# Operands of a mixer step laid out in DRAM as the core reads them: weights as packed tiles, x channel-major, vectors as columns

## The chip, the cores and the metric

The kernel runs on one core of one Trainium2 chip. A core has a matrix engine (TensorE, PE in the profile; its weight loads are PEld), a vector engine (VectorE, DVE), an activation engine (ScalarE, ACT), GpSimd (POOL) and a queue engine (SyncE, SP) that issues transfers to 16 DMA engines. All data are float32 in DRAM. The metric is device time in microseconds (us); lower is better.

## What is computed

One step of a two-layer diffusion backbone on 128 context tokens and 256 denoising tokens (384 together), width 2048. Each layer modulates a normalized x, projects it to eleven chunks of 512 channels, mixes four of the branches in different ways, gates each and projects back:

```python
shift, scale, gate = split(silu(cvec) @ w_mod[l] + b_mod[l], 3)
h = rmsnorm(x, norm_g[l]) * (1 + scale) + shift
(f_x, f_g, p_x, p_g, q, k, v, a_g, c_a, c_b, c_g) = split(h @ w_in[l], 11)
y_f = fourier_mix(f_x, w_fourier[l]) * silu(f_g)
y_p = pool_mix(p_x, w_pool[l], pool_scale[l]) * silu(p_g)
y_c = conv_module(c_a, c_b, ..., w_conv_pw[l]) * silu(c_g)
y_a = rmsnorm(diff_attention(q, k, v, lam), subln_g[l]) * silu(a_g)
x = x + gate * (concat(y_f, y_p, y_a, y_c) @ w_out[l])
```

`cvec` is `c_ctx` for the context tokens and `c` for the others. Denoising tokens attend to a cache of 128 keys and values besides their own, with rotary embedding. The outputs are the final RMS norm of both groups and the context's keys and values of both layers.

## The kernel before, in words

**Layouts.** On the chip x, h and all branches are channel-major: 128 channels on the partitions, the 384 tokens along the row, in four tiles (P, 4, 384) per tensor. Every large matmul runs as three (`mm3`, L483 to L486): weights and activations are each split into a high part in the fast float32r format and a low part with the rest (`halves`, L262; the split is an ACT copy, L113, and a DVE subtraction, L104).

**Weights.** `wtile` (L278) loads two blocks of 128 rows by 512 columns of a weight matrix as one raw tile of 512 KB, source rows of 2 KB each (`w_src`, L291), and splits it. There are five raw tiles and six high and low tiles in turn. w_mod comes three ways: `mod_item` (L304) for TensorE, in tiles (P, nk, nb, 128), one transfer for each of shift and scale, with rows of 512 bytes for one block, 1 KB for two, 2 and 4 KB for the wide ones; `side_item` (L362) for VectorE, which multiplies and adds raw rows; both are spread over the main stream by `pump` (L396) at rates set by hand (`set_rate`). In the last quarter of the output projection w_out comes in tiles (P, 8, 128), rows of 512 bytes.

**The start (L138 to L199, L838).** SP's queue is held in program order until the end of the lead stage (`manual_schedule`, closed at L881); elsewhere a planner orders every engine's instructions by priority, data flow and its own estimate of durations, and `ahead()` raises the priority of weight loads and splits. SP issues the constants' first 128 columns, two rows of conditioning vectors, then x by column groups of 512 in token-major form (two transfers a group) with norm_g and b_mod after the first group. TensorE transposes the conditioning vectors, then x block by block (48 transposes, L190), and norm_g and b_mod (L194, L195); ACT squares x with a running sum along the row (L110), DVE copies the transposes to xT (L191). The row sums give the RMS factor, which TensorE broadcasts (`bcast_tokens`, L457, matmul at L462).

**Lead stage of layer 0 (L849 to L879).** It goes through the 16 blocks of channels in groups of one, one, and then two. In each group TensorE computes shift and scale of the next (`mod_item`, matmul at L326), VectorE and ScalarE make h (`make_h`, L471), and four chunks (C_B, C_A, K, Q) get their part, added up in SBUF. x is also written to a DRAM copy `xd` (`keep_x`, L176), from which the residual is read back at the layer's end (L950). After the last group `late_vectors` (L214) loads the remaining constants and eight groups of vectors as rows and transposes them, and `make_lambda` (L238) broadcasts the lambda vectors with a matmul (L242).

**Attention's keys (`keys`, L624).** A generator that is stepped once per weight tile of the values chunk: it loads the cached keys token-major, transposes the new context keys on TensorE (L631), copies and stores them (L633, L634), transposes the cached keys (L638, L639), then rotates k and q (`rope`, L612).

**The rest.** The other chunks, the four mixers and their gates, and the output projection, where DVE adds the gated result to the residual (L107, tile xr).

Of the kernel before, what the change touches and what calls it, by code (L numbers as in the profile page):

```python
# [32 lines left out]
CONST_PARTS = [  # L33
    ("ident", 128),
    ("cdft", 256),
# [16 lines left out]
def mixer_step(  # L52
    ctx: ExitStack,
    tc: tile.TileContext,
    x_prompt, x_sample, cache_k, cache_v, c, c_ctx, norm_g, w_mod, b_mod, w_in,
    w_fourier, w_pool, pool_scale, diff_lambda, subln_g, conv_dw, conv_dw_b,
    conv_ln_g, conv_ln_b, w_conv_pw, w_out, final_g, consts,
# [39 lines left out]
    def cvtile(s):  # L97
        return cvp.tile([P, 4, 432], F32, tag="cv", name=nm(s))
# [42 lines left out]
    def load_rows(dst, rows):  # L141
        where, o = {}, 0
        for n, ap, k in rows:
            nc.sync.dma_start(out=dst[o:o + k], in_=ap)
            where[n] = o
            o += k
        return where, o
# [4 lines left out]
    load_rows(crow[:, 0:P], [("c_ctx", c_ctx.rearrange("(r p) -> r p", p=P), KC),  # L152
                             ("c", c.rearrange("o (r p) -> (o r) p", p=P), KC)])
    xtok = []
    nb = DEPTH * 3 * KC
    for g in range(4):
        xt = gtile("H", "xtok", (P, TB, BR))
        sl = slice(g * BR, (g + 1) * BR)
        nc.sync.dma_start(out=xt[:, 0, :], in_=x_prompt[0, :, sl])
        nc.sync.dma_start(out=xt[:, 1:3, :], in_=x_sample[0, :, sl].rearrange("(b p) c -> p b c", p=P))  # L160
        xtok.append(xt)
        if g == 0:
            where1, n1 = load_rows(crow[:, P:2 * P], [("norm_g", norm_g.rearrange("l (r p) -> (l r) p", p=P), DEPTH * KC)])
            nc.sync.dma_start(out=crow[:nb, 2 * P:3 * P], in_=b_mod.rearrange("l (r p) -> (l r) p", p=P))

# [1 line left out]
    cps = sm("cps")  # L167
# [6 lines left out]
    xd = [[drp.tile([P, 4, NT], F32, tag=f"xd{l}{g}", name=f"xd{l}{g}") for g in range(4)] for l in range(DEPTH)]  # L174

    def keep_x(l, g, t):  # L176
        nc.sync.dma_start(out=xd[l][g], in_=t)

    xT = []
    ssq = one.tile([P, TB, 4], F32, tag="ssq", name="ssq")  # L180
    junk = cvtile("junk").rearrange("p a b -> p (a b)")
    for g in range(4):
        xt = xtok[g]
        xT.append(gtile("X", "xT"))
# [8 lines left out]
    vps = sm("vps")  # L193
    nc.tensor.transpose(vps[:, 0:n1], crow[:n1, P:2 * P], ident[:n1, :n1])  # L194
    nc.tensor.transpose(vps[:, P:P + nb], crow[:nb, 2 * P:3 * P], ident[:nb, :nb])  # L195
    ncol = one.tile([P, n1], F32, tag="ncol", name="ncol")
    nc.vector.tensor_copy(out=ncol, in_=vps[:, 0:n1])
    bcol = one.tile([P, nb], F32, tag="bcol", name="bcol")
    nc.vector.tensor_copy(out=bcol, in_=vps[:, P:P + nb])  # L199

# [1 line left out]
    rows2 = [("final_g", final_g.rearrange("(r p) -> r p", p=P), KC),  # L202
             ("dw_b", conv_dw_b.rearrange("l (r p) -> (l r) p", p=P), 8),
             ("ln_g", conv_ln_g.rearrange("l (r p) -> (l r) p", p=P), 8),
             ("ln_b", conv_ln_b.rearrange("l (r p) -> (l r) p", p=P), 8),
             ("pscale", pool_scale.rearrange("l (r p) -> (l r) p", p=P), 8),
             ("subln", subln_g, DEPTH)]
    n2 = sum(r[2] for r in rows2)
    ndw = CONV_W * 4
    vcol = one.tile([P, n2], F32, tag="vcol", name="vcol")  # L210
    dwc = one.tile([P, DEPTH, CONV_W, 4], F32, tag="dwc", name="dwc")
    off = {}

    def late_vectors():  # L214
        nc.sync.dma_start(out=cst[:, o1:], in_=consts[:, o1:])
        vrow = kvp.tile([P, 512], F32, tag="kv", name="vrow")
        w2, _ = load_rows(vrow[:, 0:P], rows2)
        off.update(w2)
        for l in range(DEPTH):
            nc.sync.dma_start(out=vrow[:ndw, (1 + l) * P:(2 + l) * P],  # L220
                              in_=conv_dw[l].rearrange("t (b p) -> (t b) p", p=P))
        vps = sm("vps2")
        nc.tensor.transpose(vps[:, 0:n2], vrow[:n2, 0:P], ident[:n2, :n2])
        nc.vector.tensor_copy(out=vcol, in_=vps[:, 0:n2])
        for l in range(DEPTH):
            s0 = (1 + l) * P
            nc.tensor.transpose(vps[:, s0:s0 + ndw], vrow[:ndw, s0:s0 + P], ident[:ndw, :ndw])
            nc.vector.tensor_scalar(out=dwc[:, l].rearrange("p t b -> p (t b)"), in0=vps[:, s0:s0 + ndw],
                                    scalar1=0.5, scalar2=None, op0=ALU.mult)

    def col(n, i, k=1):
        return vcol[:, off[n] + i:off[n] + i + k]

# [4 lines left out]
    def make_lambda():  # L238
        lrow = gtile("X", "lrow", (P, 512))
        nc.sync.dma_start(out=lrow[0:1, :], in_=diff_lambda.rearrange("(o l) f d -> o (l f d)", o=1))  # L240
        lps = sm("lps")
# [15 lines left out]
    prio = [None]  # L257

    def ahead():
# [31 lines left out]
    def w_src(w2d, k0, c0, nk=2):  # L291
        return w2d[k0 * P:(k0 + nk) * P, c0:c0 + 512].rearrange("(k p) n -> p k n", p=P)
# [809 lines left out]
```

## Time and profile before

| | |
|---|---|
| three timed runs | 1274.0, 1268.66, 1265.95 us; median 1268.66 |
| span of the profiled execution | 1264.2 us |
| own time of the profiled execution beyond the span | not given on the page |
| mean granted TensorE clock | 0.992 |
| TensorE, VectorE, ScalarE busy | 97%, 73%, 44% |
| moved by DMA | 254.75 MB, mean 202 GB/s |

The span runs from the first to the last instruction of the profiled execution. "Busy" is the time in which an engine executes; a matmul's end is modelled, so two that overlap in the engine's pipeline count once. The chain is followed back from the last instruction, at each step to what released it.

### The profile page before, as it was taken

The numbers are of one execution on the slowest core, as the hardware profiler recorded it, in microseconds if no ns is written. First come the engines' busy times: TensorE is split into PE (matmuls) and PEld (weight loads), VectorE is DVE, ScalarE is ACT, GpSimd is POOL, SyncE is SP. The second block draws the span as 40 slices with busy tenths as digits, with TensorE's granted clock in tenths as the row PEclk, the third lists the DMA queues.
The fourth block names the chain that finished last, engine by engine and source line by source line (L and its number), as shares of the span: only waits on it lengthen the run. The fifth ranks groups of instructions, "written<-read, shape, count | busy, mean of one in ns | idle before, by whom it ended". The sixth has DMA issues, their size and how long they took to land.

```text
span 1264.2 us, 22313 instructions
## 1 busy us (share of the span) xinstructions
PE 1229.3 (97%) x8576; PEld 1144.0 (90%) x8576; DVE 923.1 (73%) x1795; ACT 557.7 (44%) x1128; POOL 2.1 (0%) x34
## 2 busy tenths in 40 slices
PE   6999999999999999999999999999999999999995
PEld 4888988798998999989998999979999999999995
DVE  4767686899995966998877559998455795657452
ACT  5422233345447545422235533334554765344442
POOL 0000000000000000000000000000000000000000
PEclk8999999999999999999999999999999999999998
DMA  9999997653446865989965444454323573545322
GB/s 273 333 314 310 297 321 268 205 183 117 140 160 201 284 233 188 315 295 310 322 212 184 154 163 150 151 160 137 121 83 110 171 253 117 184 164 188 122 69 100
DMA packets 159343, 254.75 MB, mean 202 GB/s; under 512 B 9019, under 2 KB 67973, under 8 KB 159238
## 3 DMA queue, kind: packets, MB, share of 16 engines
q1 hardware_dynamic: 159238, 253.34, 61.4%
q8 instruction: 67, 1.10, 0.4%
q14 instruction: 38, 0.31, 0.1%
HBM read 242.82 MB, written 10.49 MB: 200 GB/s over the span
## 4 chain that ended last, share of the span: by engine, by line
PE 86%; DVE 6%; DMA 4%; issue 2%; ACT 1%; SPq 1%; DVEq 0%; ACTq 0%
PE mm L484 23%; PE mm L486 22%; PE mm L485 22%; PE mod L326 4%; DVE lo L104 2%; PE mm L515 2%; PE mm L516 2%; PE mm L517 2%; DMA raw<-in_w_in_dram 2%; DVE cacc L107 1%; DMA mraw<-in_w_mod_dram 1%; PE sp L484 1%; PE sp L485 1%; PE scs L700 1%; PE sp L486 1%
## 5 line engine op out<-in xcount | busy, mean ns | idle before, releaser
L113 ACT ACTIVATE hi<-raw 128x512 fp32r<-128x512 f32 x498 | 308.5, 630 | 552.6 <-PE mm L485 341.1
L104 DVE TENSOR_TENSOR lo<-raw,hi 128x512 fp32r<-128x512 f32 x498 | 337.7, 689 | 216.0 <-ACT hi L113 203.7
L484 PE MATMUL mm<-hh,hi 128*128 128x384 f32 x1280 | 440.7, 345 | 6.6 <-DVE acc L104 3.4
L485 PE MATMUL mm<-hl,hi 128*128 128x384 f32 x1280 | 433.0, 338 | 0.0
L486 PE MATMUL mm<-hh,lo 128*128 128x384 f32 x1280 | 430.6, 339 | 0.4 <-DVE lo L104 0.4
L484 PEld LDWEIGHTS mm<-hh,hi 128*128 128x128 f32 x1280 | 240.7, 188 | 28.2 <-issue 12.2
L485 PEld LDWEIGHTS mm<-hl,hi 128*128 128x128 f32 x1280 | 242.0, 189 | 1.4 <-issue 0.8
L486 PEld LDWEIGHTS mm<-hh,lo 128*128 128x128 f32 x1280 | 241.2, 189 | 2.1 <-DVE lo L104 1.1
L484 PE MATMUL mm<-yh,hi 128*128 128x384 f32 x512 | 173.4, 340 | 3.9 <-DVE xr L107 3.9
L485 PE MATMUL mm<-yl,hi 128*128 128x384 f32 x512 | 172.4, 337 | 0.0
L486 PE MATMUL mm<-yh,lo 128*128 128x384 f32 x512 | 172.3, 337 | 0.0
L107 DVE SCALAR_TENSOR_TENSOR macc<-sraw,cmod,macc 128x512 f32<-128x512 f32 x210 | 147.7, 746 | 9.4 <-DMA sraw<-in_w_mod_dram 9.3
L107 DVE SCALAR_TENSOR_TENSOR cacc<-u,dwc,cacc 128x399 f32<-128x399 f32 x232 | 146.6, 632 | 5.3 <-ACT cacc L110 1.0
L484 PEld LDWEIGHTS mm<-yh,hi 128*128 128x128 f32 x512 | 96.2, 188 | 7.7 <-issue 6.1
L485 PEld LDWEIGHTS mm<-yl,hi 128*128 128x128 f32 x512 | 96.3, 188 | 0.0
L486 PEld LDWEIGHTS mm<-yh,lo 128*128 128x128 f32 x512 | 96.2, 188 | 0.0
L104 DVE TENSOR_TENSOR acc<-acc,mm 128x384 f32<-128x384 f32 x128 | 65.7, 552 | 24.1 <-PE mm L486 24.0
L326 PE MATMUL mod<-mraw,cmod 128*32 128x128 f32 (+2 forms) x1920 | 79.0, 294 | 3.3 <-DMA mraw<-in_w_mod_dram 2.6
L326 PEld LDWEIGHTS mod<-mraw,cmod 128*32 128x32 f32 x1920 | 48.5, 112 | 27.9 <-issue 16.0
L515 PE MATMUL mm<-hi,hh 128*128 128x512 f32 x96 | 38.4, 400 | 0.0
L516 PE MATMUL mm<-lo,hh 128*128 128x512 f32 x96 | 38.1, 397 | 0.0
L517 PE MATMUL mm<-hi,hl 128*128 128x512 f32 x96 | 37.9, 395 | 0.0
(232 smaller groups left out, 944.1 us busy)
## 6 DMA issues: line engine op xcount, KB each, us to landing
raw<-in_w_in_dram SPq DMA_DIRECT2D x172, 512.0 KB, 3.6
mraw<-in_w_mod_dram SPq DMA_DIRECT2D x72, 512.0 KB, 3.7
mraw<-in_w_mod_dram SPq DMA_DIRECT2D x128, 256.0 KB, 6.7
raw<-in_w_out_dram SPq DMA_DIRECT2D x64, 512.0 KB, 6.0
sraw<-in_w_mod_dram SPq DMA_DIRECT2D x56, 512.0 KB, 5.3
xr<-xd SPq DMA_DIRECT2D x8, 768.0 KB
xd<-xT SPq DMA_DIRECT2D x4, 768.0 KB
xd<-xr SPq DMA_DIRECT2D x4, 768.0 KB
```

What stands on the lines that cost most here:

```text
L104: (eng or nc.vector).tensor_tensor(out=out, in0=a, in1=b, op=op)
L107: nc.vector.scalar_tensor_tensor(out=out, in0=a, scalar=s, in1=b, op0=op0, op1=op1)
L113: nc.scalar.activation(out=out, in_=a, func=AF.Copy, scale=scale)
L326: nc.tensor.matmul(ps[qs, 0:nb * 32].rearrange("p (b n) -> p b n", n=32), lhsT=cmod[:, k0 + j, :], rhs=raw[:, j, :, qs], start=(k0 + j == ...
L484: nc.tensor.matmul(ps, lhsT=wh, rhs=ah, start=start, stop=False)
L485: nc.tensor.matmul(ps, lhsT=wh, rhs=al, start=False, stop=False)
L486: nc.tensor.matmul(ps, lhsT=wl, rhs=ah, start=False, stop=stop)
L515: nc.tensor.matmul(ps3[t], lhsT=hh[g][:, kb, ts], rhs=hi(j), start=st, stop=False)
L516: nc.tensor.matmul(ps3[t], lhsT=hh[g][:, kb, ts], rhs=lo(j), start=False, stop=False)
L517: nc.tensor.matmul(ps3[t], lhsT=hl[g][:, kb, ts], rhs=hi(j), start=False, stop=sp)
L700: nc.tensor.matmul(scs[qb, m][:, cs], lhsT=qs, rhs=kk[ms])
```

## The change

The host lays the operands out; the kernel's loads become plain copies. Each weight matrix becomes a flat array (`Pack`) in which the tiles stand one after the other in the order in which the program traces their loads, each tile with the bytes of a partition in one run: 4 KB per partition for a tile of 512 KB, for w_mod's shift and scale together in one transfer. x arrives channel-major (P, 4, 384) per tile. All vectors are columns of the constants, and those needed early stand with the identity matrix in the first load. The squares of x are summed over channels by TensorE with a column of ones. The DRAM copy of layer 0's x goes: its residual is read from the input. Cached keys arrive transposed, new keys leave as they stand on the chip (the host turns them), and lambda comes as 128 equal rows.

```diff
+VEC_EARLY = [("c_ctx", KC), ("c", KC), ("norm_g", DEPTH * KC), ("b_mod", DEPTH * 3 * KC)]
+VEC_LATE = [("final_g", KC), ("dw_b", 8), ("ln_g", 8), ("ln_b", 8), ("pscale", 8), ("subln", DEPTH),
+            ("dw", DEPTH * CONV_W * 4)]
-    o1 = CONST_OFF["cdft"][0]
+    o1 = CONST_OFF["ident"][0] + P
     nc.sync.dma_start(out=cst[:, :o1], in_=consts[:, :o1])
-    crow = kvp.tile([P, 512], F32, tag="kv", name="crow")
-    load_rows(crow[:, 0:P], ...)
...
+        xT.append(gtile("X", "xT"))
+        nc.sync.dma_start(out=xT[g], in_=x_in[g])
...
-    nc.tensor.transpose(cps[:, 0:2 * KC], crow[:2 * KC, 0:P], ident[:2 * KC, :2 * KC])
-    act(cmod[:, :, 0], cps[:, 0:KC], AF.Silu)
-    act(cmod[:, :, 1], cps[:, KC:2 * KC], AF.Silu)
+    act(cmod[:, :, 0], cview("c_ctx"), AF.Silu)
+    act(cmod[:, :, 1], cview("c"), AF.Silu)
+    ssq = sm("ssq")
     for g in range(4):
-        for t in range(TB):
-            act(junk[:, t * BR:(t + 1) * BR], xt[:, t, :], AF.Square, accum_out=ssq[:, t, g:g + 1])
+        xsq = gtile("M", "xsq0")
         for b in range(4):
-            ps = sm("xps")
+            act(xsq[:, b, :], xT[g][:, b, :], AF.Square)
             for t in range(TB):
-                nc.tensor.transpose(ps[:, t * P:(t + 1) * P], xt[:, t, b * P:(b + 1) * P], ident)
-            nc.vector.tensor_copy(out=xT[g][:, b, :], in_=ps[:, :NT])
+                nc.tensor.matmul(ssq[:, t:t + 1], lhsT=xsq[:, b, t * P:(t + 1) * P], rhs=ones[:, 0:1],
+                                 start=g == 0 and b == 0 and t == 0, stop=g == 3 and b == 3 and t == TB - 1)
+    dwc = cview("dw").rearrange("p (l t b) -> p l t b", l=DEPTH, b=4)
     def late_vectors():
         nc.sync.dma_start(out=cst[:, o1:], in_=consts[:, o1:])
-        vrow = kvp.tile([P, 512], F32, tag="kv", name="vrow")
...
+        nc.vector.tensor_scalar(out=cview("dw"), in0=cview("dw"), scalar1=0.5, scalar2=None, op0=ALU.mult)
     def make_lambda():
-        nc.tensor.matmul(lps, lhsT=ones[0:1, :], rhs=lrow[0:1, :])
-        lbc = gtile("X", "lbc", (P, 512))
-        nc.vector.tensor_copy(out=lbc, in_=lps)
+        lbc = kvp.tile([P, DEPTH * 4 * 64], F32, tag="kv", name="lbc")
+        nc.sync.dma_start(out=lbc, in_=lam)
-    def w_src(w2d, k0, c0, nk=2):
-        return w2d[k0 * P:(k0 + nk) * P, c0:c0 + 512].rearrange("(k p) n -> p k n", p=P)
+    def w_src(name, l, k0, c0, nk=2, n=512):
+        def rows(a):
+            return a[l, k0 * P:(k0 + nk) * P, c0:c0 + n].reshape(nk, P, n).transpose(1, 0, 2)
+        return packs[name].take(rows, (P, nk, n))
     def mod_item(l, segs, k0, nk):
...
-                nc.sync.dma_start(
-                    out=raw[:, :, o:o + n, :],
-                    in_=w_mod[l, k0 * P:(k0 + nk) * P, c0:c0 + n * P].rearrange("(k p) (b n) -> p k b n", p=P, n=P))
+            nc.sync.dma_start(out=raw, in_=packs["w_mod"].take(rows, (P, nk, nb, P)))
     def keys(l, k, q, kc):
-        ck = gtile("X", "ck", (P, 4, P))
         with ahead():
-            nc.sync.dma_start(out=ck, in_=cache_k[0, l].rearrange("h t d -> t h d"))
+            nc.sync.dma_start(out=kc, in_=cache_k[l])
         yield
-        for h in range(4):
-            nc.tensor.transpose(ps[:, h, :], k[:, h, 0:SEQ], ident)
-        ko = gtile("X", "ko", (P, 4, P))
-        nc.scalar.copy(out=ko, in_=ps)
-        nc.sync.dma_start(out=new_k[0, l].rearrange("h t d -> t h d"), in_=ko)
-        yield
-        ps = sm("ckT", (P, 4, P))
-        for h in range(4):
-            nc.tensor.transpose(ps[:, h, :], ck[:, h, :], ident)
-        nc.scalar.copy(out=kc, in_=ps)
+        nc.sync.dma_start(out=new_k[l], in_=k[:, :, 0:SEQ])
         yield
-                if k0 % 4 + nk == 4:
-                    keep_x(0, k0 // 4, xT[k0 // 4])
-            nc.sync.dma_start(out=xr[g], in_=xd[l][g])
+            nc.sync.dma_start(out=xr[g], in_=x_in[g] if l == 0 else xd[g])
+class Pack:
+    def take(self, rows, shape):
+        n = math.prod(shape)
+        flat = self.ap[self.at:self.at + n]
+        self.at += n
+        self.parts.append(rows)
+        if len(shape) == 3:
+            return flat.rearrange("(p a b) -> p a b", p=shape[0], a=shape[1])
+        return flat.rearrange("(p a b c) -> p a b c", p=shape[0], a=shape[1], b=shape[2])
```

## Rows read from the trace of the kernel before

**Rows 1.** The page: span, busy time of each engine, the chain by engine.

```profile
span 1264.2 us, 22313 instructions
...
PE 1229.3 (97%) x8576; PEld 1144.0 (90%) x8576; DVE 923.1 (73%) x1795; ACT 557.7 (44%) x1128; POOL 2.1 (0%) x34
...
PE 86%; DVE 6%; DMA 4%; issue 2%; ACT 1%; SPq 1%; DVEq 0%; ACTq 0%
...
```

**Rows 2.** Windows: stretch, us, busy us of each engine (instructions), granted clock, DMA share, GB/s.

```profile
...
2.00:4.00 2.00, 0.28 (x1) 0.18 (x1) 0.00 (x0) 1.86 (x5) 0.00 (x0) 1.00 0.42 91
4.00:8.00 4.00, 1.99 (x8) 1.59 (x9) 0.36 (x1) 1.83 (x5) 0.00 (x0) 1.00 0.87 257
8.00:12.00 4.00, 3.14 (x14) 2.14 (x13) 2.07 (x5) 2.02 (x7) 0.00 (x0) 1.00 1.00 292
12.00:14.00 2.00, 2.00 (x11) 1.50 (x10) 1.66 (x4) 1.41 (x5) 0.00 (x0) 1.00 1.06 402
14.00:20.00 6.00, 4.84 (x87) 3.47 (x85) 5.09 (x15) 4.33 (x12) 0.41 (x6) 1.00 1.20 299
28.00:31.00 3.00, 3.00 (x18) 2.56 (x20) 0.46 (x1) 1.51 (x4) 0.00 (x0) 0.50 1.15 296
66.00:74.00 8.00, 8.00 (x96) 6.97 (x96) 4.64 (x13) 3.19 (x6) 0.00 (x0) 1.00 1.05 384
...
```

**Rows 3.** Timeline of the start: start, us, engine, line, operation, count, idle before.

```profile
...
7.31 10.70 SPq L315 DMA_DIRECT2D mraw<-in_w_mod_dram  x8
...
23.54 1.08 PE L326 MATMUL mod<-mraw,cmod 128*32 128x64 f32 x32
...
24.69 0.25 DVE L331 STREAM_TRANSPOSE T<-mod 128x64 f32<-128x64 f32 x1 [4.87 <-PE mod L326]
...
27.27 0.80 PE L484 MATMUL mm<-hh,hi 128*128 128x384 f32 x3 [1.33 <-ACT hh L110]
...
```

**Rows 4.** The chain in order of time, at the start: start, us, what.

```profile
...
15.44 5.46 DMA mraw<-in_w_mod_dram
...
22.03 1.58 PE bc L462 x2
...
```

**Rows 5.** TensorE waits to 230 us (three), after (one): us total, times, longest.

```profile
...
PE mm L484 <- DVE acc L104: 3.4, 3, 1.9
PE mod L326 <- DMA mraw<-in_w_mod_dram: 0.7, 2, 0.5
PE mm L486 <- DVE lo L104: 0.4, 1, 0.4
...
PE mm L484 <- DVE xr L107: 3.9, 4, 1.6
...
```

**Rows 6.** The chain between 150 and 157 us.

```profile
...
150.37 6.41 DMA raw<-in_w_in_dram
...
```

**Rows 7.** Timeline of TensorE around the transposes of layers 0 and 1.

```profile
...
224.47 0.40 PE L515 MATMUL mm<-hi,hh 128*128 128x512 f32 x1
...
226.56 0.48 PE L516 MATMUL mm<-lo,hh 128*128 128x512 f32 x1
...
229.96 0.66 PE L638 MATMUL ckT<-cst,ck 128*128 128x128 f32 x4
...
827.43 0.60 PE L631 MATMUL kT<-cst,k 128*128 128x128 f32 x4
...
```

**Rows 8.** Squares by tile (ns min/median/max); row sums and broadcast on the chain.

```profile
...
L110 ACT ACTIVATE xsq<-xr x30: 507/524/527, 561.8 to 1250.8; 128x384 f32<-128x384 f32 x30
...
673.97 0.83 PE st L467 x6
...
676.65 0.86 PE bc L462 x2
...
```

**Rows 9.** Layer 1: SP after the key store; landing of the values' store.

```profile
...
829.81 10.07 SPq L266 DMA_DIRECT2D raw<-in_w_in_dram  x3
...
DMA to landing us min/median/max: 4.5/4.5/4.5
...
```

More of the change, by code (lines that the diff above doesn't have):

```diff
@@ L54, in mixer_step @@
     tc: tile.TileContext,
[L55 to L57 removed]
+    x_in, cache_k, cache_v, consts, lam, packs,
     y_prompt, y_sample, new_k, new_v,
@@ L154, in mixer_step @@
-    xtok = []
-    nb = DEPTH * 3 * KC
-    for g in range(4):
[L157 to L164, printed above, removed]
@@ L171, in mixer_step @@
     warm = one.tile([P, 1], F32, tag="warm", name="warm")
     act(warm, cmod[:, 0, 2:3], AF.Sqrt, bias=eps_t[:, 0:1])
[L174 to L181, printed above, removed]
+    ncol = cview("norm_g")
+    bcol = cview("b_mod")
+    xd = [drp.tile([P, 4, NT], F32, tag=f"xd{g}", name=f"xd{g}") for g in range(4)]
@@ L193, in mixer_step @@
[L193 to L207, printed above, removed]
@@ L215, in late_vectors @@
         nc.sync.dma_start(out=cst[:, o1:], in_=consts[:, o1:])
-        vrow = kvp.tile([P, 512], F32, tag="kv", name="vrow")
[L217 to L229, printed above, removed]
+        nc.vector.tensor_scalar(out=cview("dw"), in0=cview("dw"), scalar1=0.5, scalar2=None, op0=ALU.mult)
     def col(n, i, k=1):
-        return vcol[:, off[n] + i:off[n] + i + k]
+        return cview(n)[:, i:i + k]
@@ L311, in mod_item, with rows @@
         with ahead():
-            o = 0
-            for kind, b0, n in segs:
-                c0 = MOD.index(kind) * D + b0 * P
-                nc.sync.dma_start(
-                    out=raw[:, :, o:o + n, :],
-                    in_=w_mod[l, k0 * P:(k0 + nk) * P, c0:c0 + n * P].rearrange("(k p) (b n) -> p k b n", p=P, n=P))
-                o += n
+            def rows(a):
+                parts = []
+                for kind, b0, n in segs:
+                    c0 = MOD.index(kind) * D + b0 * P
+                    parts.append(a[l, k0 * P:(k0 + nk) * P, c0:c0 + n * P].reshape(nk, P, n, P))
+                import numpy as np
+                return np.concatenate(parts, axis=2).transpose(1, 0, 2, 3)
+            nc.sync.dma_start(out=raw, in_=packs["w_mod"].take(rows, (P, nk, nb, P)))
         key = (l, segs)
@@ L370, in side_item @@
         with ahead():
-            nc.sync.dma_start(out=raw, in_=w_src(w_mod[l], k0, c0))
+            nc.sync.dma_start(out=raw, in_=w_src("w_mod", l, k0, c0))
         for j in range(2):
@@ L531, in small_proj @@
         ah, al = src
-        wt = [wtile(w_src(src2d, 2 * kt, 0)) for kt in range(2)]
+        wt = [wtile(w_src(name, l, 2 * kt, 0)) for kt in range(2)]
         for b in range(4):
@@ L811, in pool_proj @@
             yield
-        hi, lo = wtile(w_pool[l].rearrange("g c d -> c g d"), shape=(P, 4, P))
+        hi, lo = wtile(packs["w_pool"].take(lambda a: a[l].transpose(1, 0, 2), (P, 4, P)), shape=(P, 4, P))
         for g in range(4):
@@ L834, in evac4 @@
         return t
-    ssum = tiny.tile([P, TB], F32, tag="ssum", name="ssum")
-    nc.vector.tensor_reduce(out=ssum, in_=ssq, axis=AX.X, op=ALU.add)
-    stat = ssum
+    stat = ssq[:, 0:TB]
     for l in range(DEPTH):
@@ L932, in mixer_step @@
         mix_p = gtile("M", "mixp")
-        ft = start(small_proj(w_fourier[l], fm, lambda b, ps: nc.scalar.copy(out=mix_f[:, b, :], in_=ps), WF))
+        ft = start(small_proj("w_fourier", l, fm, lambda b, ps: nc.scalar.copy(out=mix_f[:, b, :], in_=ps), WF))
         pt = start(pool_proj(l, px, mix_p))
@@ L941, in mixer_step @@
         mix_c = gtile("M", "mixc")
-        ct = start(small_proj(w_conv_pw[l], cs, lambda b, ps: nc.scalar.copy(out=mix_c[:, b, :], in_=ps), WC))
+        ct = start(small_proj("w_conv_pw", l, cs, lambda b, ps: nc.scalar.copy(out=mix_c[:, b, :], in_=ps), WC))
         gate(C_G, Y_C, mix_c, ct)
@@ L1068, in shape_constants, with __init__, array, channel_columns @@
     parts["edge"] = np.broadcast_to(edge.reshape(1, 64), (P, 64))
[L1069 to L1076 removed]
+    return parts
+WEIGHTS = ("w_in", "w_mod", "w_out", "w_fourier", "w_pool", "w_conv_pw")
+_OUTS = [((1, SEQ, D), "float32"), ((1, DEC, D), "float32"), ((DEPTH, P, 4, SEQ), "float32"),
+         ((DEPTH, SEQ, BR), "float32")]
+class Pack:
+    def __init__(self, ap, size):
+        self.ap, self.size, self.at, self.parts = ap, size, 0, []
+    def take(self, rows, shape):
+        n = math.prod(shape)
+        assert self.at + n <= self.size
+        flat = self.ap[self.at:self.at + n]
[4 more added lines that the diff above has]
+        return flat.rearrange("(p a b c) -> p a b c", p=shape[0], a=shape[1], b=shape[2])
+    def array(self, a):
+        import numpy as np
+        assert self.at == self.size
+        return np.concatenate([np.ascontiguousarray(rows(a)).ravel() for rows in self.parts])
+def channel_columns(i):
+    import numpy as np
+    def cols(a):
+        return np.asarray(a, np.float32).reshape(-1, P).T
+    parts = {"c_ctx": cols(i["c_ctx"]), "c": cols(i["c"]), "norm_g": cols(i["norm_g"]), "b_mod": cols(i["b_mod"]),
+             "final_g": cols(i["final_g"]), "dw_b": cols(i["conv_dw_b"]), "ln_g": cols(i["conv_ln_g"]),
+             "ln_b": cols(i["conv_ln_b"]), "pscale": cols(i["pool_scale"]), "subln": cols(i["subln_g"]),
+             "dw": cols(i["conv_dw"])}
+    parts.update(shape_constants())
+    return np.ascontiguousarray(np.concatenate([parts[n] for n, _ in CONST_PARTS], axis=1).astype(np.float32))
 def kernel(**inputs):
```

86 lines of the change are left out of this document (37 added, 49 removed).

## The prediction

> **What bounds the kernel now.** I read the page's busy shares and chain first. The reader sees a TensorE that is busy for 97% of a 1264.2 us span and makes up 86% of the chain that ended last, against 6% for VectorE and 4% for DMA [rows 1]. Only what shortens TensorE's own work, or the time in which it has nothing to do, can shorten this kernel.
>
> Then I asked where TensorE has nothing to do. The timeline of the start shows the first matmul of the main stream at 27.27 us [rows 3]; what runs before it are small matmuls and transposes between waits. After it, the table of TensorE's waits shows only 4.5 us between 28 and 230 us (3.4 + 0.7 + 0.4), and its longest row in all the rest is 3.9 us, behind VectorE's residual update [rows 5]. So the start is the one large gap: 27 us in which the main stream does not run.
>
> The chain through the start runs through DMA: w_mod tiles (mraw) on their way from 15.44 to 20.90 us [rows 4], then the mod matmuls, the transposition T, the first h, and the first main matmul. The windows say how fast the transfers go: 91 GB/s from 2 to 4 us, 292 from 8 to 12, 402 from 12 to 14 where 2 KB rows of x pass, 299 from 14 to 20 where, by the load's own shape, all are 512-byte rows of w_mod; all of these from 8 us on at a DMA share of 1.00 or more. Later, with rows of 1 and 2 KB mixed with the 6 KB rows of the x copies, 384 GB/s [rows 2].
>
> **The change part by part.**
>
> *Start (gain 6.9 us, from 2.7 to 8.2).* Until the first main matmul the same bytes must come: constants 0.15 MB (288 columns of 512 bytes), x 4 x 786 KB = 3.15 MB, four mod tiles of 524 KB = 2.10 MB; together 5.39 MB. Today the last of them passes at about 21.4 us: the windows of rows 2 from 2 to 20 us add up to 4.98 MB, and the rest follows at the 299 GB/s of the last one. After the change there are five issues on the SP queue before the first mod tile (constants, four of x) instead of thirteen, and four issues for the four tiles instead of the eight that hold SP from 7.31 us for 10.70 us [rows 3]. Each partition's piece of a tile is 4 KB (mod) or 6 KB (x) in one run. I take 390 GB/s, between the 384 and the 402 of rows 2, and a full stream from 2.3 us, as soon as the first transfers appear in the row of 2 to 4 us: 2.3 + 5.39/0.390 = 16.1 us, and 0.5 us for the last piece to land and be seen (my estimate). The fourth tile's matmuls take 1.08 us [rows 3], to 17.7; from T to the first main matmul it is 27.27 - 24.69 = 2.6 us [rows 3], to 20.3 or 20.4 us. That is 6.9 us sooner. Lower bound: no faster than 299 GB/s, 2.3 + 18.0 + 0.5 + 1.1 + 2.7 = 24.6, gain 2.7. Upper: 402 GB/s, mod matmuls in 0.65 us, 19.0, gain 8.2.
>
> The other path into the first h, the token sums, must not be later. The squares of x are now 16 instructions on ScalarE at 0.524 us [rows 8], four per tile of x, 2.1 us, about the time in which a tile of 786 KB passes (2.0 us). After each square three matmuls, priced as the six of the st group in 0.83 us [rows 8]: 0.14 us each, 0.42 us per square, under ScalarE's pace. The last x is there at 2.3 + 3.30/0.390 + 0.5 = 11.3; sums at 13.9; root, reciprocal and three diagonal tiles about 2 us; broadcast 0.86 [rows 8] to 1.58 us at the lower clock [rows 4]; copy 0.5: about 17.3 to 18.0 us. It meets the mod path and costs nothing, or some tenths. The 48 transposes and 16 VectorE copies that go were beside the transfers, and give nothing of their own.
>
> *Clock (0, from -1.5 to +1.7).* From 28 to 31 us the granted clock is 0.50, the lower level of 1.2 GHz, after a start in which TensorE was busy only in part (4.84 of 6 us from 14 to 20) [rows 2]. Three us at half the rate cost 1.5 us. Whether the new start has one less or one more I can't read from a trace of the old one; I take the same.
>
> *Stream of weights, 28 to 230 us (gain 4, from 0 to 4.5).* The chain before the waits of VectorE's acc and lo runs back into a weight tile: raw from w_in, 6.41 us on its way at 150.37 [rows 6]. The DMA share is 1.05 in the stretch of this stage in rows 2, with rows of 1 and 2 KB. With 4 KB runs the same bytes take less, and the x copies to DRAM of layer 0 (four of 786 KB) fall away. TensorE can regain no more than its waits, 4.5 us [rows 5]; I take 4, since the chain ends with VectorE work in line that stays.
>
> *Transposes that go (gain 3.4, from 2.5 to 4.5).* From 224.47 to 226.56 TensorE does one main matmul (0.24 us) and the lambda broadcast, the vector transposes and kT: 1.85 us. The cached-key transposes at 229.96 are busy 0.66 us, of which I count 0.6, one more vector transpose 0.1. In layer 1 kT at 827.43 is busy 0.60 us, of which some 0.15 overlaps the next matmul (estimate); ckT the same: 0.9 us. Sum 3.4 [rows 7]. These stand between full-speed matmuls, so all of it comes back.
>
> *The rest (gain 0.5, from 0 to 2).* In the last quarter of the output projection, and in the side sums of w_mod, rows of 512 bytes and 2 KB become 4 KB. TensorE's waits after 230 us are mostly on VectorE (3.9 us on the residual, four times [rows 5]), which is 73% busy overall and keeps its work; I give the transfers 0.5 us of it. Smaller vector copies on VectorE and ScalarE go; both are off the chain there.
>
> *What it adds.* New keys leave straight from k, and the rotation later writes other columns of that tile. If it waited for the store, VectorE's splits behind it would wait too, and TensorE for them; a store of this size lands in 4.5 us [rows 9], and the rotation's own write is the last of its steps, some 5 us later in program order. I take 0; the upper price stands with the rivals. The in-place halving of the convolution weights is one VectorE instruction in place of two. Lambda now arrives as 128 rows, 256 KB instead of 2 KB, on a queue at that point below its limit: 0.
>
> Sum: 6.9 + 0 + 4 + 3.4 + 0.5 = 14.8 us off the span, 1264.2 to 1249.4. The page gives the profiled execution no time beyond its span; the median of the three timed runs, 1268.66, is 4.46 us above that span. So 1268.66 - 14.8 = 1253.9; I say 1254.
>
> A rule of the Trainium skill speaks against the start's term: its page "DMA: Bandwidth & Descriptors", section Specifications, gives 512 B as the smallest transfer at line rate, so 512-byte rows would lose nothing to 4 KB. The trace disagrees as far as rows 2 go: 299 GB/s at 512 bytes against 384 to 402 with longer rows. By that rule the rival called "no faster" below would hold.
>
> **The rivals.**
>
> *No faster transfers.* If a full DMA share moves about 300 GB/s for other reasons than the row length, the last mod tile still comes at about 20.3 to 21 us. For it: the share is 1.20 at 299 GB/s, so the engines have more than one packet open and something else may hold them. Against it: 402 GB/s at a share of 1.06. Gain then: start 2.7, transposes 3.4, stream 0 to 1: 6.6 us, 1262.
>
> *Given back.* Data flow and priorities give the planner another order on every engine, from its own idea of how long a transfer takes. The start comes sooner, but mod matmuls are cut into more pieces, or VectorE, the next engine, is late elsewhere. Start and transposes give 10.3; a return of 4 us and none of the 4 us of waits: 6 us, 1262.5. For it: VectorE stands before nearly all remaining TensorE waits [rows 5].
>
> *Slower: the key store blocks the rotation.* SP issues in order; just where the key store of layer 1 would stand, three raw loads hold SP for 10.07 us [rows 9]. If the store is put behind such loads and the rotation waits for the whole tile, VectorE stands for up to 10.07 + 4.5 = 14.6 us a layer, 29 us in two, with the splits of w_in queued behind. Less the gain of 14.8 that is 14 us slower: 1283. It decides from about 15 us of standing in both layers together that TensorE has no split tiles left to cover. Against it: k is complete long before the store, today's is issued at once, and the two touch different columns.
>
> *More.* No dip of the clock, 402 GB/s and all waits gone: 8.2 + 1.5 + 4.5 + 4.5 + 2 = 20.7, 1248.
>
> **How the numbers follow.** Forecast (gain of 11 to 18) 0.55; no faster 0.17; given back 0.15; more 0.07; slower 0.06. A measurement of this kernel can tell about 1% from no change (the three runs lie within 0.6%); 1% is 12.7 us, just inside the forecast's own spread. Faster by over 1% takes the larger part of the forecast, about 0.50 of its 0.55, and "more" 0.07: 0.57. Slower by over 1% is most of the last rival: 0.05. The rest, 0.38, is within 1%. For 8 in 10 the range runs from 1246, two below "more", since timed runs spread by some us, to 1264, which holds both weak rivals.
>
> **What would show it.** First main matmul near 20 us (right), at 24 or later (no faster transfers); GB/s of 380 to 400 between 4 and 16 us; TensorE's waits between its start and the values chunk under 1 us; none of the lines of rows 7 left; TensorE busy less by the transposes alone, the rest of the gain in idle time. VectorE waiting on a key store, or SP held before it, would show the slower rival. The forecast is wrong if TensorE's idle time after 30 us grows by what the start gains.

## The result, and the profile after

| | before | after |
|---|---|---|
| timed runs, median | 1269.38 us (1265.95 to 1274.0, 10 runs) | 1262.01 us (1259.06 to 1266.68, 10 runs) |
| ratio of the two, 95% interval | | 0.9941 (0.9926 to 0.9956) |
| span of the profiled execution | 1264.2 us | 1260.0 us (own time 1261.78) |

The change makes the kernel 0.6% faster, 7.4 us by the medians: within the 1% that counts as no change here. The forecast was 14.8 us. The profile of before fits its fastest timed run, so the two traces differ by only 4.2 us; the stages below are read from these two.

The page of after, first the span and busy times, then the chain that ended last by engine:

```profile
span 1260.0 us, 22153 instructions
...
PE 1232.5 (98%) x8600; PEld 1155.2 (92%) x8600; DVE 912.3 (72%) x1773; ACT 553.7 (44%) x1116; POOL 2.1 (0%) x34
...
PE 92%; DVE 3%; DMA 2%; ACT 1%; issue 1%; SPq 0%; DVEq 0%; ACTq 0%
```

Against [rows 1], DMA and VectorE lost half their share of the chain and TensorE took it: 92% for 86%. TensorE's busy time should have fallen by the transposes that went. It rose, from 1229.3 to 1232.5 us. Something on TensorE was added that costs more than they did.

The timeline of TensorE in the first 36 us of after (start, us, engine line operation, count, idle before):

```profile
6.80 19.36 PE L166 MATMUL ssq<-ones,xsq 128*128 128x1 f32 x90 [6.80 <-ACT xsq L112]
26.09 0.44 PE L271 MATMUL mod<-mraw,cmod 128*32 128x64 f32 x8
26.46 1.44 PE L166 MATMUL ssq<-ones,xsq 128*128 128x1 f32 x6
27.84 1.72 PE L271 MATMUL mod<-mraw,cmod 128*32 128x64 f32 x56
29.48 1.65 PE L407 MATMUL bc<-dg,ones 128*128 128x384 f32 x2
31.06 1.34 PE L271 MATMUL mod<-mraw,cmod 128*32 128x64 f32 x64
32.79 0.65 PE L271 MATMUL mod<-mraw,cmod 128*32 128x64 f32 x32 [0.38 <-DVE T L276]
35.06 1.33 PE L429 MATMUL mm<-hh,hi 128*128 128x384 f32 x3 [1.62 <-ACT hh L112]
```

Here is the answer. The token sums (ssq) and eight mod matmuls among them hold TensorE without a gap from 6.80 to 27.9 us, and the other mod matmuls and the broadcast bc queue behind them. The program asks for 48 such matmuls (16 squares, three column groups of 128 tokens); the trace has 90 + 6 = 96 records, two per matmul, at 19.36/90 = 0.215 us each. The first main matmul starts at 35.06 us, not at the 20.4 forecast, and 7.8 us later than before [rows 3].

The transfers had done their part long before. Windows of after, columns as in [rows 2]:

```profile
2.00:4.00 2.00, 0.00 (x0) 0.00 (x0) 0.00 (x0) 1.59 (x3) 0.00 (x0) 1.00 0.95 183
4.00:8.00 4.00, 1.20 (x6) 1.20 (x6) 0.00 (x0) 2.09 (x6) 0.00 (x0) 1.00 1.01 415
8.00:12.00 4.00, 4.00 (x21) 4.00 (x20) 0.00 (x0) 3.60 (x9) 0.00 (x0) 1.00 1.00 417
...
14.00:20.00 6.00, 6.00 (x30) 6.00 (x30) 0.00 (x0) 0.98 (x1) 0.00 (x0) 1.00 0.80 313
20.00:27.00 7.00, 7.00 (x40) 6.81 (x40) 0.00 (x0) 0.00 (x0) 0.00 (x0) 1.00 0.01 2
```

The first column of figures after the length is TensorE's busy time, the last is GB/s. The bytes come at 415 to 417 GB/s against 257 and 292 in the same stretches of [rows 2]. From 20 to 27 us there is nothing left to move (2 GB/s): TensorE's sums hold up everything.

One reading of these windows is a trap. They show a granted clock of 1.00 until 31 us, but bc takes 1.65 us there, as at the lower level in [rows 4] (1.58), and 0.86 at full clock [rows 8]. The trace of after has no clock record before 31.6 us, so the column shows 1.00 for want of one. The sums ran at 1.2 GHz: e6 below has the same sums at both levels, and shows these passes at the lower one.

The stages come from the times at which the same matmuls start in both traces:

| stage, by TensorE's first matmul of each | before | after | forecast |
|---|---|---|---|
| start, to the first main matmul | 27.27 us | 35.06 us (+7.8) | -6.9 |
| from there to the first values matmul of layer 0 | 183.21 | 178.98 (-4.2) | -4.0 |
| values matmul to first scores of layer 0 | 43.61 | 40.25 (-3.4) | -2.5 |
| scores to output projection of layer 0 | 269.21 | 269.46 (+0.2) | 0 |
| output projection to first main matmul of layer 1 | 156.09 | 152.28 (-3.8) | -0.5 with all the rest |
| layer 1 to its output projection | 430.10 | 429.20 (-0.9) | -0.9 |
| output projection of layer 1 and the end | 154.71 | 154.77 (+0.1) | 0 |
| sum | | -4.2 | -14.8 |

In the values stage TensorE is busy for the whole of both traces (43.61 and 40.25 us), so the 3.4 us there are work that went. TensorE's waits in after from 35 to 240 us, and the last row of those after 240 us (us in total, times, longest):

```profile
PE mm L429 <- ACT hh L112: 2.0, 2, 1.6
PE mm L429 <- DVE acc L106: 1.3, 1, 1.3
PE mm L431 <- DVE lo L106: 0.4, 1, 0.4
...
PE mm L429 <- DVE xr L109: 0.3, 1, 0.3
```

Of [rows 5], the wait on mraw is gone and acc has fallen from 3.4 to 1.3 us; the wait on the residual xr has fallen from 3.9 to 0.3. The transposes of keys in [rows 7] have no counterpart in after, nor have the broadcast of lambda and the transposes of vectors.

Of the stage from the first main matmul to the values matmul, windows with the same columns, before and then after:

```profile
27.27:210.48 183.21, 178.68 (x1825) 158.79 (x1825) 133.07 (x295) 61.12 (x119) 0.00 (x0) 0.99 0.93 309
35.06:214.04 178.98, 176.62 (x1824) 159.15 (x1825) 133.62 (x304) 61.14 (x120) 0.00 (x0) 0.99 0.83 303
```

TensorE's idle time in it falls from 4.5 to 2.4 us. That is half of the stage's 4.2 us; the other 2.1 us are busy time, which falls with the same matmuls, and why it does was not followed.

### The profile page after: what moved, and what is told of

It reads as the page before. It is cut to its first block, busy times and chain, and to the rows that moved or that the text cites. A ratio compares the mean times of both kernels' runs of the same rounds, so it can differ in the third digit from the quotient of the medians.

```text
span 1260.0 us, 22153 instructions
## 1 busy us (share of the span) xinstructions
PE 1232.5 (98%) x8600; PEld 1155.2 (92%) x8600; DVE 912.3 (72%) x1773; ACT 553.7 (44%) x1116; POOL 2.1 (0%) x34
## 4 chain that ended last, share of the span: by engine, by line
PE 92%; DVE 3%; DMA 2%; ACT 1%; issue 1%; SPq 0%; DVEq 0%; ACTq 0%
PE mm L429 25%; PE mm L430 23%; PE mm L431 23%; PE mod L271 5%; PE mm L460 2%; PE mm L461 2%; PE mm L462 2%; PE ssq L166 2%; DVE lo L106 1%; DMA raw<-in_w_in_dram 1%; PE sp L430 1%; PE sp L429 1%; PE scs L634 1%; PE sp L431 1%; PE aso L658 1%; PE fb L701 1%
## 5 line engine op out<-in xcount | busy, mean ns | idle before, releaser
L429 PEld LDWEIGHTS mm<-hh,hi 128*128 128x128 f32 x1280 | 241.0, 188 | 26.7 <-issue 11.4
L109 DVE SCALAR_TENSOR_TENSOR cacc<-u,cst,cacc 128x399 f32<-128x399 f32 x232 | 146.5, 631 | 7.6 <-ACT cacc L112 3.2
L112 ACT ACTIVATE hh<-ht,AB 128x128 fp32r<-128x128 f32 x64 | 26.9, 450 | 25.8 <-DVE ht L109 25.6
```

What stands on the lines that cost most here:

```text
L109: nc.vector.scalar_tensor_tensor(out=out, in0=a, scalar=s, in1=b, op0=op0, op1=op1)
L112: nc.scalar.activation(out=out, in_=a, func=func, **kw)
L429: nc.tensor.matmul(ps, lhsT=wh, rhs=ah, start=start, stop=False)
```

## The experiments

The theory: the change's gains all came, and the token sums took most of them back, by the number of TensorE's passes times a pass at the lower clock. The rivals: the late start costs nothing in itself, since weight tiles pile up behind it and the stream then catches up, so that the gains of the middle are only the other side of it; or the packed weights give nothing and the gains come from elsewhere. Each of the first four kernels ran beside the kernel before on one chip (median 1267.17 us, 11 runs).

**e1_dve_sums.** After, with the 16 squares added up by VectorE, so that TensorE does three token sums instead of 48.

```diff
+    xacc = None
...
-            for t in range(TB):
-                nc.tensor.matmul(ssq[:, t:t + 1], lhsT=xsq[:, b, t * P:(t + 1) * P], rhs=ones[:, 0:1],
...
+            if xacc is None:
+                xacc = xsq[:, b, :]
+            else:
+                tt(xacc, xacc, xsq[:, b, :], ALU.add)
+    for t in range(TB):
+        nc.tensor.matmul(ssq[:, t:t + 1], lhsT=xacc[:, t * P:(t + 1) * P], rhs=ones[:, 0:1],
+                         start=t == 0, stop=t == TB - 1)
```

> The changed kernel, but the squares of x are added up by VectorE (15 additions, 0.55 us each) and only three token sums are left to TensorE. Theory (the 48 token sums hold the start; the other gains of the change are its own): first main matmul at 20 to 22 us instead of 35.1, the values chunk of layer 0 begins at about 200 us instead of 214, time about 1248 us, 14 below the changed kernel. Rival (the lead stage ran fast after the change only because weights had piled up during the late start): first main matmul at 20 to 22 us too, but the values chunk begins at 208 us or later and the time is 1256 to 1262.

Measured: 1251.03 us (1250.47 to 1253.14), ratio 0.987 (0.9856 to 0.9884). Timelines of its start, VectorE's line first, then TensorE's:

```profile
8.55 7.85 DVE L106 TENSOR_TENSOR xsq<-xsq,xsq 128x384 f32<-128x384 f32 x12
...
16.45 1.44 PE L171 MATMUL ssq<-ones,xsq 128*128 128x1 f32 x6 [2.62 <-DVE xsq L106]
17.82 1.93 PE L275 MATMUL mod<-mraw,cmod 128*32 128x64 f32 x62
19.68 1.65 PE L411 MATMUL bc<-dg,ones 128*128 128x384 f32 x2
...
25.18 0.80 PE L433 MATMUL mm<-hh,hi 128*128 128x384 f32 x3 [1.22 <-ACT hh L112]
```

The first main matmul comes at 25.18 us, 9.9 sooner than in after; the first values matmul at 203.06 (11.0 sooner), the end at 1248.7 (11.3 sooner). So the time lost at the start is kept to the end: the rival of the piled-up weights falls. The start itself misses its expectation of 20 to 22 us. In the trace VectorE's adds, 7.85/12 = 0.65 us each, are slower than the squares of [rows 8] (0.524 us), and the last three sums, the mod matmuls and bc still run at the lower clock (1.65 us for bc); what each of these costs was not separated.

**e2_fp32r_sums.** After, with the 48 sums in the one-pass float32r format; the squares are rounded to it, which changes the sums by that rounding.

```diff
+    onesr = one.tile([P, 2], F32R, tag="onesr", name="onesr")
+    nc.vector.tensor_copy(out=onesr, in_=ones[:, 0:2])
-        xsq = gtile("M", "xsq0")
+        xsq = gtile("M", "xsq0", dt=F32R)
-                nc.tensor.matmul(ssq[:, t:t + 1], lhsT=xsq[:, b, t * P:(t + 1) * P], rhs=ones[:, 0:1],
+                nc.tensor.matmul(ssq[:, 2 * t:2 * t + 2], lhsT=xsq[:, b, t * P:(t + 1) * P], rhs=onesr,
...
```

> The changed kernel with the squares rounded to float32r, so that each of the 48 token sums is one pass of TensorE instead of two. Theory (the price is the passes, 0.215 us each): the sums end about 10 us sooner, first main matmul at 24 to 26 us, time about 1252. If the price is not in the passes but in the wait for x or for the squares, the sums end where they did and the time stays at 1262. The rival of piled-up weights: first main matmul at 24 to 26, time 1258 or more.

Measured: 1251.39 us (1250.81 to 1252.0), ratio 0.987 (0.9857 to 0.9883); the sums on TensorE's timeline:

```profile
6.16 9.76 PE L168 MATMUL ssq<-onesr,xsq 128*128 128x2 f32 x45 [6.16 <-ACT xsq L112]
```

One record per matmul, 9.76/45 = 0.217 us, the same as a float32 pass. Half as many passes take half the time, and the first main matmul comes at 24.05 us, as expected. What costs is the pass, not the number format. Each pass loads 128 columns of weights (128x128 in every weight-load record) to multiply one or two columns with them.

**e3_packs_only** and **e4_rows_new_start** split the change in two: before with packed weights alone, and after with weights in rows as before, all else of the change kept (the cached and new values too, which the change also lays out as they stand on the chip). The diff is that of e3 against the kernel before; e4 is the same edit backwards on the kernel after.

```diff
-    def w_src(w2d, k0, c0, nk=2):
-        return w2d[k0 * P:(k0 + nk) * P, c0:c0 + 512].rearrange("(k p) n -> p k n", p=P)
+    def w_src(name, l, k0, c0, nk=2, n=512):
...
+        return packs[name].take(rows, (P, nk, n))
...
-            for kind, b0, n in segs:
-                nc.sync.dma_start(
-                    out=raw[:, :, o:o + n, :],
-                    in_=w_mod[l, k0 * P:(k0 + nk) * P, c0:c0 + n * P].rearrange("(k p) (b n) -> p k b n", p=P, n=P))
...
+            nc.sync.dma_start(out=raw, in_=packs["w_mod"].take(rows, (P, nk, nb, P)))
```

> The kernel before with the packed weights alone: x, vectors, keys and lambda as before, transposes kept. Theory: the mod tiles land sooner, first main matmul at 22 to 24 us (27.3 before); lead stage about 4 us and last quarter of layer 0's output projection about 4 us shorter; time about 1258, some 11 below before. Rival (row length gives nothing): first main matmul at 27, time within 2 us of before.

> The changed kernel with the weights back in their row-major arrays. Theory: first main matmul at 35 us or a little later, behind the token sums as in the changed kernel; no gain in the lead stage from the transfers beyond what piled up, none in the output projection; transposes of keys and lambda still gone (4 us): time 1270 to 1274, at or above before. Rival (most of the gain comes from the removed transposes and not from the weights): time about 1262, as the changed kernel.

Measured: e3 1255.5 us (1254.27 to 1256.55), ratio 0.99 (0.9887 to 0.9913); e4 1273.24 (1270.74 to 1275.05), ratio 1.0041 (1.0026 to 1.0056). The two parts add up: -1.0% and +0.4% make the -0.6% of the change. Without the packed weights the change makes the kernel 0.4% slower, little but clear of the noise. Windows of e3, for the stretches of [rows 2] in which w_mod passes:

```profile
14.00:20.00 6.00, 5.04 (x99) 3.74 (x103) 4.98 (x15) 4.87 (x12) 0.42 (x6) 1.00 1.03 409
66.00:74.00 8.00, 8.00 (x59) 7.37 (x58) 6.73 (x18) 2.94 (x7) 0.00 (x0) 1.00 1.03 415
```

In before these were 299 GB/s at a DMA share of 1.20 and 384 at 1.05. This is the fair test of the rival "no faster transfers", with the same program around it: 409 against 299 GB/s. The packing changes three things at once, though: the length of the rows, their distance in DRAM, and the number of transfers (one of 512 KB in place of two of 256 KB). The number is not needed for the slow rate: from 630 to 635 us before moves 309 GB/s at a share of 1.18, nearly all its packets under 2 KB, with w_out's tiles in single transfers of 512 KB. Length and distance were not separated. The rule of the Trainium skill weighed in the prediction (page "DMA: Bandwidth & Descriptors", section Specifications) is not borne out here: rows of 512 bytes moved at 0.73 of the rate of 4 KB runs.

e3 gains 2.7 us at the start (first main matmul 24.57), 2.5 more up to the values chunk, 2.5 in the output projection of layer 0, and 1.6 in layer 1. The total is as expected, the stages named in the expectation are smaller. e4's time is as its theory had it. The 1.6 us of layer 1 are not the packs': e7 and e8 below, with w_mod or w_out packed, take 430.0 and 430.1 us there, as before. What differs is the clock, 0.50 from 680 to 683 us in before and 1.00 in the same place in e3.

In its profiled run, one of its slower, e4 loses 7.1 us at the start and 5.8 in that output projection. Its TensorE waits 5.8 us on xr in place of 3.9, and only 2.0 us of the 5.8 lost are idle time; the other 3.8 are busy time, in a stage in which the clock fell twice. Windows of e4, the stage first:

```profile
527.24:689.15 161.91, 154.15 (x1106) 146.96 (x1102) 132.06 (x243) 52.07 (x92) 0.35 (x6) 0.97 0.80 268
567.00:570.00 3.00, 3.00 (x11) 3.00 (x10) 3.00 (x9) 1.52 (x3) 0.00 (x0) 0.50 0.50 143
608.00:614.00 6.00, 5.32 (x17) 5.35 (x18) 6.00 (x15) 2.09 (x4) 0.00 (x0) 0.50 0.96 322
```

In before the stage has TensorE busy for 150.31 us at 1.00. In e4 it idled for more than 2 us on the residual just before each of the two falls, and then worked at the lower level.

The next four ran on another chip (before 1270.0 us, 17 runs).

**e5_pair_sums.** After, with pairs of squares added by VectorE into float32r and 24 one-pass sums (so the sums carry that rounding).

```diff
+        xpr = gtile("H", "xpr", (P, 2, NT), F32R)
...
+            if b % 2:
+                tt(xpr[:, b // 2, :], xsq[:, b - 1, :], xsq[:, b, :], ALU.add)
+                for t in range(TB):
+                    nc.tensor.matmul(ssq[:, 2 * t:2 * t + 2], lhsT=xpr[:, b // 2, t * P:(t + 1) * P], rhs=onesr,
...
```

> The changed kernel with squares added in pairs by VectorE into float32r, then 24 token sums of one pass instead of 48 of two. Theory (the start is the time to x plus what TensorE's sums need): sums end at about 14.5 us, first main matmul at 21 to 22 us, time 1247 to 1249, two or three below the run with VectorE's sums alone (1251). Rival (from here the mod tiles and the lower clock set the start): first main matmul at 24 to 25 us, time 1250 to 1252.

Measured: 1250.34 us (1248.64 to 1252.74), ratio 0.9839 (0.9816 to 0.9863): the fastest of all, though its interval overlaps that of e1. TensorE's timeline at its start:

```profile
14.72 0.80 PE L171 MATMUL ssq<-onesr,xpr 128*128 128x2 f32 x3
...
16.86 1.65 PE L411 MATMUL bc<-dg,ones 128*128 128x384 f32 x2
...
22.57 1.02 PE L433 MATMUL mm<-hh,hi 128*128 128x384 f32 x3 [1.62 <-ACT hh L112]
23.39 0.52 PE L434 MATMUL mm<-hl,hi 128*128 128x384 f32 x1
```

The sums end at 15.5 us and the first main matmul comes at 22.57, 2.6 us sooner than in e1: between what the theory (21 to 22) and its rival (24 to 25) expected; the time is in the rival's range (1250 to 1252). From the end of the sums to the first main matmul it is 7.1 us here, 7.0 in e2, 7.3 in e1 and 7.2 in after, so in these four the end of the sums sets the start. But bc (1.65 us) and the first main matmuls (0.52 us, against 0.34 later) still run at the lower clock, up to 26.4 us, and in the profiled run, its slowest, the lead over e1 is gone by the output projection (514.68 us, e1 512.67). Where it goes was not followed further.

**e6_warm.** After, with 18 matmuls of ones by ones ahead of the sums, whose result nothing uses.

```diff
+    dum = sm("dum")
+    for _ in range(18):
+        nc.tensor.matmul(dum[:, 0:P], lhsT=ones, rhs=ones, start=True, stop=True)
```

> The changed kernel with 18 matmuls of ones on ones ahead of the token sums, whose result nothing reads, in the time before x comes. Theory (a pass of a token sum takes 0.215 us at the start and 0.138 us later because TensorE is at the lower clock there): the passes fall to 0.14 us or near it, the sums end about 7 us sooner, first main matmul at 27 to 29 us, time about 1255. Rival (a lone pass of this kind takes that long at the start whatever came before): 0.215 us as before, first main matmul at 35 us, time 1262.

Measured: 1259.26 us (1257.85 to 1260.58), ratio 0.9914 (0.989 to 0.9938). Windows of the sums alone (after the length: TensorE's matmuls, its weight loads, ScalarE; clock, DMA share, GB/s):

```profile
7.00:11.00 4.00, 4.00 (x38) 4.00 (x38) 0.00 (x0) 1.00 1.00 417
12.00:16.00 4.00, 4.00 (x21) 4.00 (x20) 0.00 (x0) 0.50 1.02 402
16.00:20.00 4.00, 4.00 (x20) 4.00 (x21) 0.00 (x0) 0.50 0.60 232
```

This run has clock records from 4.6 us on, before its first sum. A window also counts the passes that cross its edges; by the starts of the records, two passes stand 0.112 us apart at 1.00 and 0.213 us apart at 0.50, and 0.213 us in all of after's sums, with the transfers running or gone. So the price at the lower clock is shown. The dummy matmuls, which stream 128 columns, have the same two distances, so the one column of a sum is not what costs.

There is also a thing that I had not expected: the clock fell to 0.50 at 11.4 us while TensorE was busy for all of the window, with these sums. The first main matmul came at 31.32 us, later than the 27 to 29 expected and 3.7 sooner than in after, where 96 passes at 0.112 in place of 0.213 us would have saved 9.7.

**e7_wmod_packed**, **e8_wout_packed.** Before, with only w_mod (the first two edits), or only w_out (the last two), packed as in the change.

```diff
+    def w_pack(name, l, k0, c0, nk=2, n=512):
...
+            nc.sync.dma_start(out=raw, in_=packs["w_mod"].take(rows, (P, nk, nb, P)))
...
+            nc.sync.dma_start(out=raw, in_=w_pack("w_mod", l, k0, c0))
...
-                    hi, lo = wtile(w_src(w_out[l], 2 * kt, g * BR))
+                    hi, lo = wtile(w_pack("w_out", l, 2 * kt, g * BR))
...
+                        hi, lo = wtile(w_pack("w_out", l, k0, c0, 8, P), shape=(P, 8, P))
```

> The kernel before with w_mod alone packed (rows of 512 bytes, 1 and 2 KB become 4 KB). Theory (the rows under 2 KB cost; those of 2 KB hardly): most of the start and lead gains of the packed weights, time 1259 to 1262, 5 to 8 below before. Rival (the gain is spread over all weights by bytes): w_mod is 101 of 226 MB, 5 us, and the start does not move.

> The kernel before with w_out alone packed (rows of 512 bytes in the last quarter of the output projection, of 2 KB elsewhere). Theory: layer 0's output projection 2 to 4 us shorter, start and lead unchanged, time about 1264, 3 below before. Rival (the gain there came from the side sums' rows of w_mod): nothing, 1267.

Measured: e7 1261.84 us (1260.91 to 1263.88), ratio 0.9937 (0.9917 to 0.9956), with 4.1 us gained by the values chunk, of which 1.4 at the start (not clear of the noise: e8 and e9, which leave the start as it was, reach the first main matmul at 26.05 and 26.93 us, and the values chunk 0.3 and 0.7 us later than before); e8 1265.99 (1258.27 to 1268.29, 12 runs), ratio 0.9961 (0.9943 to 0.9979). Together they make the 1.0% of e3, which leaves nothing that can be measured for w_in, whose rows were 2 KB, and the small matrices. The window from 66 to 74 us says the same: 408 GB/s in e7, 375 in e8, 384 before. For e8 the profiled run, its slowest, shows no gain at the output projection (156.81 us for 156.09, with the clock at 0.57 from 563 to 567 us), so the stage in which its 0.4% arises stays open.

**e9_keys_only.** Before, with the cached keys loaded as they lie in a transposed cache and new keys stored as they stand on the chip: only kT, ckT and their copies go (on a third chip; before 1269.52 us, 17 runs).

```diff
-        ck = gtile("X", "ck", (P, 4, P))
...
-            nc.tensor.transpose(ps[:, h, :], k[:, h, 0:SEQ], ident)
...
-        nc.sync.dma_start(out=new_k[0, l].rearrange("h t d -> t h d"), in_=ko)
+        nc.sync.dma_start(out=new_k[l], in_=k[:, :, 0:SEQ])
```

> The kernel before with the key cache transposed in DRAM and the new keys stored as they stand, nothing else: 16 transposes and four ScalarE copies go. Theory (TensorE's time there comes back in full): about 1.3 us in layer 0 and 0.9 us in layer 1, 2.2 us together, time about 1267 where before is 1269; VectorE's first rotation does not wait on the key store. Rival (the store blocks the rotation): a wait of several us of VectorE's rope line on the store, time 1275 or more.

Measured: 1265.31 us (1264.1 to 1271.88, 12 runs), ratio 0.9976 (0.9957 to 0.9994), about 3 us, and 0.8 to 5.5 by the interval; the four groups of transposes come to some 2.5 us by [rows 7] (2 x 0.66 and 2 x 0.60). In the trace the values stage of layer 0 is 1.8 us shorter (41.86 for 43.61). VectorE's waits, in e9 as in after, have no row in which it waits for a key store: the slower rival did not occur.

## Why the prediction was wrong

**The step that failed** is in the start's term: "After each square three matmuls, priced as the six of the st group in 0.83 us [rows 8]: 0.14 us each", and with it "It meets the mod path and costs nothing, or some tenths". The sums were to end at 13.9 us and ended at 27.9. Three things were wrong in it.

First the count. The six records of st in [rows 8] are three matmuls, each of two passes: the step's own code says three (one per 128 tokens), and the same reading of x2 under bc, a single matmul with two records, stood in [rows 4] and [rows 8] beside it. So 0.83 us is 0.28 us per matmul. With that alone the 48 sums would have taken 13.3 us, to 20.1 us at best, and from the sums' end to the first main matmul it is 35.06 - 27.9 = 7.2 us: 27.3 us, the very start of before. The start's term would have been 0, and the sum 7.9 us. That this is near the 7.4 measured is chance, as the next points show: the start lost 7.8 us, and other stages gave more than forecast.

Second the clock. I wrote 0 for it, thinking of the three us after the start, and priced bc at either level but the sums at full clock only. They ran at the lower, 0.43 us per matmul: 20.8 us (19.36 + 1.44) in place of the 6.7 that 48 x 0.14 makes. Of these 14.1 us the count makes 6.6 by the row's price and the clock 7.5; by e6's 0.112 us between two passes at full clock, the split is 4.1 and 10.0. Together they are nearly all of the 14.7 by which the first main matmul missed its forecast. A rule of the Trainium skill would have given a price for the pass: the page "TensorE: Matmul & The Clock Gate", section "LDWEIGHTS (loading the stationary operand)", lets a load of 128 columns take 128/1.2 ns. That is an estimate of 0.107 us per pass; e6 shows 0.112 at full clock and 0.213 at half.

Third the engine. "The 48 transposes ... were beside the transfers, and give nothing" fits the trace of before, where the transposes ended at 17.4 us and TensorE still waited for a mod tile until 21.0. But the 48 sums that took their place were taken to be beside the transfers as well. In after the transfers stopped before 20 us, and the sums outlived them by 8 us and more. With weights in rows (e4) the first main matmul comes at 34.41 us, so it is not the faster transfers that made the sums late. A path that "meets" another after the change was not given a bound of its own, and the range of the start's term ended at a gain of 2.7 us. It should have ended at a loss.

**What held.** The transfers: 390 GB/s was assumed, 415 to 417 came at the start, where x passes, and e3 and e7 (409 GB/s from 14 to 20 us in both) show what the packing of w_mod alone does. The transposes: 3.4 forecast, 4.3 measured (3.4 in layer 0, 0.9 in layer 1). No cost for the key store, for lambda or for the halved weights shows in the waits.

**What held in number only.** The stream of weights: 4 us forecast, 4.2 measured. It was to come out of TensorE's waits, which could give no more than their 4.5 us; the waits on acc and mraw did fall, but the idle time by only 2.2 us, and 2.1 us came from busy time that the forecast did not have. Its own sign, waits under 1 us in that stage, was missed (1.3 + 0.4).

**What was too small.** The rest was given 0.5 us, with TensorE's late waits "mostly on VectorE". The output projection of layer 0 gave 3.8: TensorE's wait on xr fell from 3.9 to 0.3 us. e3 gets 2.5 of it with packed weights alone, so these waits hung on the transfers, at least in part, although the releaser shown is VectorE. The stage varies between runs of kernels that don't differ there (e1 -2.5; e9, with rows, +1.5), and I don't put it down to one matrix.

**The rivals.** Two of them named the measured time with the wrong mechanism, "no faster transfers" (1262) and "given back" (1262.5). Transfers were faster, and nothing was returned later: the loss came at the start, before the stream. The range for 8 in 10, to 1264, was drawn to hold both, and so it holds the measured time. e1 puts the sum to the test: with the sums' work off TensorE, and all else of the change in place, the gain is 1267.17 - 1251.03 = 16.1 us by the medians and 15.5 by the traces, against 14.8 forecast. By its stages it is 2.1 us at the start, 5.3 in the stream, 3.3 and 2.4 in the values stage and in layer 1, and 2.5 in the output projection. So the total is right in part by luck: the start is 4.8 us smaller than thought, and the clock, which the forecast left as it was, helped. Before and after run at 0.50 for some 3 us behind the first main matmul of either layer; in the trace of e1 the clock is 1.00 there (25 to 29 and 666 to 670 us), and its layer 1 takes 427.66 us against 429.20 in after, with the same transposes gone.

## What to carry to other kernels

Before a price is taken from a row, count the program's calls against the row's records: a float32 matmul is two, and one with a single streamed column costs as much as one with 128. An operation that moves from an engine with time to the one that bounds the kernel needs its own end time at both clock levels, with the queue behind it; "beside the transfers" holds only as long as the transfers last, and the same change had made them shorter. Let the engine that idles add up what it can, and give TensorE few column sums (three in e1, 24 of one pass in e5, for 48 of two): e1 and e5 make the 0.6% into 1.3% and 1.6%.

## What the runs showed of the hardware

A pass of TensorE with a 128x128 weight load and one or two streamed columns takes 0.112 us at full clock (e6) and 0.213 us at half, in float32 (two per matmul: after, e6) and float32r (one: e2) alike; with 128 streamed columns in float32 it takes the same (the dummy matmuls of e6).

The granted clock fell from 1.00 to 0.50 in e6 while TensorE's records were busy without a gap, and in after the same sums, without a gap from 6.8 to 27.9 us, ran at the lower level to their end. So a busy TensorE does not by itself get or keep the full clock. Nor does the same wait always lose it: ahead of layer 1 TensorE waits 1.9 us for h in before, e1 and e3, and behind it the clock is 0.50 in before and 1.00 in e1 and e3. Where it fell, layer 1 took 1.5 to 1.6 us longer (430.1 against 428.5 with the transposes, 429.2 against 427.7 without), so a gain of this size between two traces should be checked against the clock first. The clock is not all that moves this stage: e6, at 1.00 as well, took 428.6 us.

And the clock column of a window before the first record of the trace says 1.00 whatever the clock was; the length of a known matmul (bc: 0.86 or 1.6 us) tells it.
